# The sample's queries meet their states in eight columns per sequence, its scores in 64 columns

## The chip, the core and the metric

The kernel runs on one core of one Trainium2 chip. The metric is the device time of one execution in microseconds (us); the time of a kernel is the median of several runs. On a core several engines work side by side, each through its own instruction stream in order: TensorE (PE; its weight loads, PEld, are told apart from its matmuls in the profile), VectorE (DVE), ScalarE (ACT), GpSimd (POOL) and SyncE (SP), which here issues the DMA transfers. They wait for each other by semaphores.

## The reference: what is computed

One layer of a decoder, for a prompt of 2048 tokens and for a sample of 8 sequences with 8 new tokens each, with the same weights: a norm, one input projection, two kinds of linear recurrence (four heads of retention, four heads of HGRN2, all 128 x 128), a norm and a gate for each head, an output projection, a squared-ReLU MLP, and a last norm. The recurrences work chunk by chunk:

```python
b = jnp.cumsum(gb, axis=2)
...
A = jnp.einsum('bhtd,bhsd,bhtsd->bhts', qb, kb, decay)
o = jnp.einsum('bhts,bhsv->bhtv', A, vb) + jnp.einsum('bhtd,bhdv->bhtv', qb * jnp.exp(b), S)
...
S_new = S * jnp.exp(b_last[:, :, 0, :])[..., None] + jnp.einsum('bhsd,bhsv->bhdv', k_dec, vb)
```

An output has two terms: the scores of a token against the tokens of its own chunk, times their values, and its query times the state from before the chunk. The prompt starts from a state of zeros and hands it on from chunk to chunk. Each sample sequence starts from a state of its own (`state_ret`, `state_hgrn`: 8 sequences x 4 heads of 128 x 128 for each kind), which its 8 tokens alone meet; its scores are those of its 8 tokens among themselves.

## The kernel before

**Groups.** The tokens go through in three groups, `GROUPS`: 512 of the prompt; the 64 of the sample with 768 of the prompt; 768 of the prompt. Only the second has sample tokens (`g.ns` = 64), in columns 0 to 63 of its 832; features lie on the partitions. For each group come the mixer (`mix`: for each of the four heads p the gates of the head before, then `project`, `mixer`, `values`), the output projection and the MLP.

**Precision.** The large matmuls split each operand in two parts (hi, lo) of a reduced type and take three products; `cut` and `parts` make the parts on ACT (L359, L498) and DVE (L360, L499). The matmuls of the recurrence take 32-bit operands as they are; in the profile each such matmul stands as two weight loads and two matmuls, called passes here.

**Tiles.** `slab` is a pool of 42 buffers of 128 x 832, from which nearly all intermediate results come (`get`); `ld` are six buffers that DMA fills. In PSUM there are two double banks `pj` for projections and four banks `mm` (which also hold `po`, the outputs of the heads). A buffer is given out again when its last reader is done, and its next writer waits for that.

**Order.** `tick()` is called after every few projection matmuls, and runs what is due by then. `mixer` puts the recurrence's steps on that agenda, so that they stand between the projection's matmuls in TensorE's stream. From the order in which the program is written, the framework's scheduler makes the final order of each engine's stream and gives out buffers; so an edit can move instructions that it does not name.

**The sample's part, for each of the four heads of the second group.** Retention's scores: `ret_scores(2)` multiplies all 128 first columns of keys and queries (L962) into a bank and masks them on DVE with a table that is zero outside the sample (L963). HGRN2's: `kept(i, ..., 2)` does the same for the level of 4 tokens (L850, L851); other levels come from shared sums (`own`, `next_to`, `quad`). `turn` transposes keys (L788) and empties the bank on ACT (L790, or with a scale L792). `sample_load` fetches four states in each of two `ld` buffers (L744), and `sample_queries` copies the queries: `g.qm` are two slabs, set to zero once at the start of `mix` (L618); sequence s has 128 columns, of which its 8 queries fill those of its own tokens (columns 8 s to 8 s + 7), and the rest stay zero. `sample_out` adds nine matmuls into the bank `po`: the values times the scores (L756), and for each sequence its state times its 128 columns (L759). As the columns of other sequences are zero, the sum puts each sequence's term in its own place. `sample_update` then makes the new states (L770 on DVE, L773 on PE, L777 or L779 and L780), and they are stored (L781). Other lines named below: `exponents`, `decays` and `decayed` (L832, L833, L837, L843, L844), `corners` (L913, which use a part of the array's columns), `values` (L727), projections (L352), `residual` (L1159).

## Time and profile before

| | us |
|---|---|
| median of 3 runs | 2588.03 |
| lowest and highest run | 2586.77, 2589.51 |
| the profiled execution | 2586.12 |
| its span, first to last instruction | 2584.3 |
| TensorE matmuls busy in the span | 2538.6 |
| VectorE, ScalarE, GpSimd busy | 1688.4, 1166.5, 772.3 |

The profile is of one execution. Matmul rows of the trace name the output and inputs, the part of the array that is used (128*128 is all: rows*columns), and the output's size. Matmuls are pipelined: a row's length is not the time that the matmul takes from the next one. The distance of starts tells that, and a weight load that starts late shows that PE had to wait for something. Where an engine idles, the row in brackets says how long and what ended it.

### The profile page before, as it was taken

What the parts mean: (1) busy time and instruction counts of PE and PEld (TensorE: products, weight loads), DVE (VectorE), ACT (ScalarE), POOL (GpSimd) and SP (SyncE); (2) the same over time, 40 slices, a digit from 0 to 9 for tenths busy, and PEclk for the clock granted to TensorE, in tenths of its full rate; (3) what the DMA queues carried; (4) which work ended last, traced back from release to release, by engine and by line L of the source; (5) the groups of instructions that cost most, each with busy time, mean ns of one, the idle gap of its engine ahead of it and who ended that gap; (6) DMA issues with size and microseconds to landing.
All of it is one profiled execution on the core that took longest, in us unless ns stands there. A gap on an engine that the chain in (4) does not pass through costs nothing. (4 is left out here: it accounts for less than half of the span.)

```text
span 2584.3 us, 37190 instructions
## 1 busy us (share of the span) xinstructions
PE 2538.6 (98%) x14689; PEld 2404.1 (93%) x14689; DVE 1688.4 (65%) x2122; ACT 1166.5 (45%) x1575; POOL 772.3 (30%) x480
## 2 busy tenths in 40 slices
PE   8999999999999999999999999999999999999997
PEld 6888788888999999999999999999999999999997
DVE  6666776556666576646655977875556465559886
ACT  6666533234434343345434444454444354345443
POOL 5655251111234143201222322242244012223222
PEclk9999999999999999999999999999999999999999
DMA  7556755554264655613456555442222325565452
GB/s 256 207 201 210 279 202 195 192 195 161 98 220 158 225 202 170 230 72 136 167 169 228 206 174 177 149 160 82 99 108 100 120 90 179 183 218 194 171 180 82
DMA packets 146237, 442.33 MB, mean 171 GB/s; under 512 B 14736, under 2 KB 36240, under 8 KB 146064
## 3 DMA queue, kind: packets, MB, share of 16 engines
q1 hardware_dynamic: 145920, 439.94, 48.8%
q8 instruction: 116, 1.90, 0.3%
q14 instruction: 57, 0.47, 0.1%
q10 hardware_dynamic: 144, 0.02, 0.0%
HBM read 331.11 MB, written 108.79 MB: 170 GB/s over the span
## 5 line engine op out<-in xcount | busy, mean ns | idle before, releaser
L352 PE MATMUL pj<-slab,hi 128*128 128x416 f32 (+2 forms) x2844 | 742.4, 364 | 6.3 <-ACT hi L277 5.9
L277 ACT CAST hi<-raw 128x1024 fp32r<-128x1024 f32 x330 | 346.7, 1051 | 677.9 <-PE pu L1145 191.6
L292 POOL TENSOR_TENSOR lo<-raw,hi 128x1024 fp32r<-128x1024 f32 x119 | 314.7, 2645 | 933.9 <-ACT hi L277 866.4
L352 PEld LDWEIGHTS pj<-slab,hi 128*128 128x128 f32 x2844 | 514.3, 189 | 39.1 <-ACT hi L277 5.9
L1145 PE MATMUL pd<-slab,hi 128*128 128x416 f32 (+1 forms) x1792 | 469.5, 342 | 5.1 <-DVE slab L1588 3.1
L352 PE MATMUL pj<-slab,lo 128*128 128x416 f32 (+2 forms) x1422 | 435.6, 364 | 0.1
L1145 PE MATMUL pu<-slab,hi 128*128 128x416 f32 (+1 forms) x1600 | 408.1, 342 | 0.0
L292 DVE TENSOR_TENSOR lo<-raw,hi 128x1024 fp32r<-128x1024 f32 x211 | 269.5, 1277 | 188.7 <-ACT hi L277 188.2
L1145 PEld LDWEIGHTS pd<-slab,hi 128*128 128x128 f32 x1792 | 329.4, 188 | 8.7 <-DVE slab L1588 3.7
L1145 PE MATMUL pd<-slab,lo 128*128 128x416 f32 (+1 forms) x896 | 307.9, 344 | 0.0
L1145 PEld LDWEIGHTS pu<-slab,hi 128*128 128x128 f32 x1600 | 294.0, 188 | 1.5
L352 PEld LDWEIGHTS pj<-slab,lo 128*128 128x128 f32 x1422 | 259.9, 189 | 17.2 <-issue 1.9
L1145 PE MATMUL pu<-slab,lo 128*128 128x416 f32 (+1 forms) x800 | 264.2, 343 | 0.0
L352 PE MATMUL mm<-slab,hi 128*128 128x512 f32 x740 | 229.5, 390 | 0.0
L727 PE MATMUL pjv<-hi,slab 128*128 128x256 f32 x1088 | 211.9, 286 | 1.0 <-ACT slab L737 1.0
L1344 DVE TENSOR_TENSOR slab<-slab 128x832 fp32r<-128x832 f32 (+1 forms) x144 | 162.9, 1148 | 37.4 <-ACT slab L1340 18.1
L727 PEld LDWEIGHTS pjv<-hi,slab 128*128 128x128 f32 x1088 | 174.2, 190 | 3.0 <-ACT slab L737 1.4
L1340 ACT CAST slab<-slab 128x832 fp32r<-128x832 f32 (+1 forms) x144 | 122.0, 860 | 116.7 <-DVE slab L1351 83.1
L1145 PEld LDWEIGHTS pd<-slab,lo 128*128 128x128 f32 x896 | 168.1, 188 | 0.5
L352 PEld LDWEIGHTS mm<-slab,hi 128*128 128x128 f32 x740 | 138.5, 188 | 29.2 <-ACT slab L1175 0.4
L727 PE MATMUL pjv<-lo,slab 128*128 128x256 f32 x544 | 153.8, 283 | 0.0
L1145 PEld LDWEIGHTS pu<-slab,lo 128*128 128x128 f32 x800 | 149.7, 188 | 0.5
(205 smaller groups left out, 3708.3 us busy)
## 6 DMA issues: line engine op xcount, KB each, us to landing
raw<-w SPq DMA_DIRECT2D x270, 512.0 KB, 4.1
u<-ld SPq DMA_DIRECT2D x32, 416.0 KB, 4.2
slab<-u SPq DMA_DIRECT2D x32, 416.0 KB, 5.7
u<-ld SPq DMA_DIRECT2D x32, 384.0 KB, 4.6
slab<-u SPq DMA_DIRECT2D x32, 384.0 KB, 4.9
ld<-x SPq DMA_DIRECT2D x16, 416.0 KB, 4.8
ld<-x SPq DMA_DIRECT2D x16, 384.0 KB, 4.0
raw<-su1S SPq DMA_DIRECT2D x8, 512.0 KB, 3.9
```

The source lines that it names most:

```text
L277: self.nc.scalar.copy(hi, raw)
L292: eng.tensor_tensor(out=lo, in0=self.second.pop(j), in1=hi.bitcast(F32), op=ALU.subtract)
L352: self.nc.tensor.matmul(pj[:, i, :T2], w, a[:, c0:c1], start=j == 0 and q == 0, stop=j == n - 1 and q == 2)
L727: nc.tensor.matmul(pj[:, i * 256:(i + 1) * 256], a[:, s:s + C], ww, start=kb == 0 and q == 0, stop=kb == KB - 1 and q == 2)
L1145: self.nc.tensor.matmul(*a, **k)
L1340: self.nc.scalar.copy(hi[:, :g.T], B[name][:, :g.T])
L1344: self.nc.vector.tensor_tensor(out=lo[:, :g.T], in0=B[name][:, :g.T], in1=hi.bitcast(F32)[:, :g.T], op=ALU.subtract)
```

## The change

The mixer's slabs of zeros `g.qm`, their memsets and `sample_queries` are gone. `sample_out` takes the queries where they are: for each sequence one matmul of its state (128 columns of weights, as before) with its 8 query columns, into the 8 columns of `po` that are its own. The first matmul of `sample_out` takes the 64 sample tokens alone: 64 partitions of values and scores, 64 columns. The two kinds of scores, L850 and L962, are made for 64 x 64, and masked on 64 partitions and 64 columns. The number of matmuls stays the same. The line numbers in this document are those of the kernel before, for both kernels, unless it says otherwise.

```diff
@@ mix
-        if g.ns:
-            g.qm = [self.get(), self.get()]
-            for q in g.qm:
-                nc.gpsimd.memset(q, 0.0)
@@ sample_queries, sample_out
-    def sample_queries(self, g, q):
-        for i in range(2):
-            z = g.qm[i][:, 32 * i:32 * i + 4 * 136].rearrange("p (s r) -> p s r", r=136)[:, :, 0:SLEN]
-            self.nc.gpsimd.tensor_copy(z, q[:, 32 * i:32 * i + 32].rearrange("p (s r) -> p s r", r=SLEN))
-
-    def sample_out(self, g, po, v, AT, s0):
+    def sample_out(self, po, v, AT, s0, q):
         nc = self.nc
-        nc.tensor.matmul(po[:, 0:P], v, AT, start=True, stop=False)
-        for i in range(2):
-            for s in range(4):
-                nc.tensor.matmul(po[:, 0:P], s0[i][:, s * P:(s + 1) * P], g.qm[i][:, s * P:(s + 1) * P],
-                                 start=False, stop=i == 1 and s == 3)
+        nc.tensor.matmul(po[:, :NS], v[:NS], AT[:NS, :NS], start=True, stop=False)
+        for s in range(NSEQ):
+            c = slice(s * SLEN, (s + 1) * SLEN)
+            nc.tensor.matmul(po[:, c], s0[s // 4][:, s % 4 * P:(s % 4 + 1) * P], q[:, c], start=False, stop=s == NSEQ - 1)
@@ kept, sg == 2
-                ps = self.mm(P)
-                nc.tensor.matmul(ps, qk[:, :P], qk[:, :P], start=True, stop=True)
-                nc.vector.copy_predicated(self.ATs, msk[:, NLV + i], ps)
+                ps = self.mm(NS)[:NS]
+                nc.tensor.matmul(ps, qk[:, :NS], qk[:, :NS], start=True, stop=True)
+                nc.vector.copy_predicated(self.ATs[:NS, :NS], msk[:NS, NLV + i, :NS], ps)
@@ ret_scores, sg == 2
-                x["ats"] = self.get()[:, :P]
-                ps = self.mm(P)
-                nc.tensor.matmul(ps, rk[:, :P], rq[:, :P], start=True, stop=True)
-                nc.vector.tensor_tensor(out=x["ats"], in0=ps, in1=con[:, C_RS + p * P:C_RS + (p + 1) * P], op=ALU.mult)
+                x["ats"] = self.get()[:, :NS]
+                ps = self.mm(NS)[:NS]
+                nc.tensor.matmul(ps, rk[:, :NS], rq[:, :NS], start=True, stop=True)
+                nc.vector.tensor_tensor(out=x["ats"][:NS], in0=ps, in1=con[:NS, C_RS + p * P:C_RS + p * P + NS], op=ALU.mult)
@@ mixer
         def sample_load(hd):
             x["s0", hd] = self.sample_states(hd, p)
-            self.sample_queries(g, q if hd else rq)
...
-                self.sample_out(g, x["po", 0][0], b["vs"][0], x["ats"], x["s0", 0])
+                self.sample_out(x["po", 0][0], b["vs"][0], x["ats"], x["s0", 0], rq)
...
-                self.sample_out(g, x["po", 0][1], b["vs"][1], self.ATs, x["s0", 1])
+                self.sample_out(x["po", 0][1], b["vs"][1], self.ATs, x["s0", 1], q)
```

## The prediction

> **What bounds the kernel now.** I read the page's head, then the stretch in which the second group is mixed, then TensorE's waits in it. The first fence has the span and busy times of the page and the clock by core; the second the busy time of 640 to 1085 us (columns: length, then busy us and instructions of PE, PEld, DVE, ACT, POOL, clock, DMA share, GB/s); the third what TensorE waited for there (us in all, times, longest).

> ```profile
> span 2584.3 us, 37190 instructions
> PE 2538.6 (98%) x14689; PEld 2404.1 (93%) x14689; DVE 1688.4 (65%) x2122; ACT 1166.5 (45%) x1575; POOL 772.3 (30%) x480
> core 0: 2584.3 us, clock 0.997
> ```
> ```profile
> 640.00:1085.00 445.00, 438.24 (x2849) 419.16 (x2848) 301.44 (x447) 181.63 (x267) 147.20 (x118) 1.00 0.54 185
> ```
> ```profile
> PE mm L505 <- DVE slab L360: 3.3, 2, 1.6
> PE mm L788 <- ACT slab L792: 1.4, 1, 1.4
> PE mm L970 <- DVE AT L877: 1.1, 1, 1.1
> PE pjv L727 <- ACT slab L737: 1.0, 2, 0.6
> ```

> TensorE is the bound: 438.2 of 445.0 us busy at full clock, and the 6.8 us of waits are the four rows. So an edit counts by what it does to the time between matmul starts on PE, and by what it does to those four waits. Work taken from POOL (147 us busy of 445) or DVE (301 of 445) counts only where PE waits for it.

> **What the change touches on POOL, DVE and the queues.** The groups of these lines from 620 to 1090 us (count, then busy us in all, mean ns, idle us before):

> ```profile
> L752 POOL COPY slab<-slab 128x32 f32<-128x32 f32 x16 | 4.8, 315 | 29.7 <-PE po L759 29.1 <-DMA sd11S<-raw 0.3
> L618 POOL MEMSET slab<- 128x832 f32 x2 | 1.5, 791 | 17.6 <-PE mm L352 17.6
> L851 DVE COPY_PREDICATED ATs<-msk,mm 128x128 f32<-128x128 uint8 x4 | 1.2, 295 | 0.0
> L963 DVE TENSOR_TENSOR slab<-mm,con 128x128 f32<-128x128 f32 x4 | 1.2, 292 | 4.8 <-PE mm L962 4.8
> ```

> The 16 copies and two memsets go: 6.3 us of POOL, with 29.7 and 17.6 us idle ahead of them, and no row above has PE waiting for POOL: nothing. The eight DVE instructions on a quarter of the elements save at most their 2.4 us, beside PE: nothing. No DMA is added. In the changed program's order one of the two loads of retention states for each of the second to fourth heads is issued behind the stores of the head before:

> ```profile
> L744 SPq DMA_DIRECT2D ld<-ret_s x8: 378/380/380, 634.2 to 973.2; - x8
> L759 PE MATMUL po<-slab,ld x128: 275/275/275, 752.9 to 1079.3; 128*128 128x128 f32 x128
> ```

> The last of these loads starts at 973 us for a use after 1070: the cover is some 90 us, and a step of a few us is hidden. The two slabs that come free matter for one wait, below.

> **The eight-column matmuls (L759).** Each matmul of this type is two passes, each with its own weight load (128 rows for 64 matmuls). The timeline (start us, length, engine, line, count) of one call in the first head:

> ```profile
> 752.52 0.38 PEld L756 LDWEIGHTS po<-slab 128*128 128x128 f32 x2
> 752.82 1.87 PEld L759 LDWEIGHTS po<-slab,ld 128*128 128x128 f32 x16
> 754.60 0.30 PEld L352 LDWEIGHTS pj<-slab,lo 128*128 128x128 f32 x2
> ```

> From 752.82 to the next line's load at 754.60 are 1.78 us for 16 passes: 0.111 us each. The change cuts the moving columns from 128 to 8, and leaves the weights at 128 columns. Whether a pass can be shorter than 0.111 depends on what a weight load takes when nothing hides it. The corners (L913) show it, the one place where the array works on fewer columns (128*64 and 128*32 against 128*128):

> ```profile
> 714.93 0.28 PE L727 MATMUL pjv<-hi,slab 128*128 128x256 f32 x1
> 715.14 0.42 PEld L913 LDWEIGHTS mm<-slab 128*64 128x64 f32 x6
> 715.63 0.19 PEld L727 LDWEIGHTS pjv<-hi,slab 128*128 128x128 f32 x1
> 715.63 0.39 PE L727 MATMUL pjv<-hi,slab 128*128 128x256 f32 x1
> 715.74 0.19 PEld L727 LDWEIGHTS pjv<-lo,slab 128*128 128x128 f32 x1
> 715.85 0.28 PE L727 MATMUL pjv<-lo,slab 128*128 128x256 f32 x1
> ...
> 721.13 0.45 PEld L913 LDWEIGHTS mm<-slab 128*32 128x32 f32 x12
> ```
> ```profile
> L913 PE MATMUL mm<-slab 128*32 128x32 f32 x256 | 13.3, 204 | 3.0 <-DVE slab L971 3.0
> L913 PEld LDWEIGHTS mm<-slab 128*32 128x32 f32 x256 | 10.6, 117 | 10.2 <-issue 5.2 <-DVE slab L971 3.4 <-ACT slab L837 0.3
> L913 PEld LDWEIGHTS mm<-slab 128*64 128x64 f32 x128 | 9.2, 137 | 5.0 <-issue 1.8 <-DVE slab L844 1.1
> ```

> At 715.63 a load of 128 columns starts with the array empty. Its matmul is recorded 0.39 long instead of 0.28, and the load after it starts at 715.74: 0.11 us of bare load. With one length of a load taken off, the passes of 64 columns are (0.42 - 0.137) / 5 = 0.057 us apart, those of 32 (0.45 - 0.117) / 11 = 0.030. The corners move as many columns as they load, so these two alone don't tell load from stream; the bare load does. Bounds of the new pass: 0.030 (stream alone) to 0.111; I take 0.108, by the bare load of the same 128 columns. 128 x (0.111 - 0.108) = 0.4 us saved, at most 128 x 0.081 = 10.4 us.

> [...]

> **The 64-wide scores (L850, L962).** Their output is now 64 partitions, so the array works as 128*64 for two passes, amid 128*128 work. The fence above shows what such a visit costs: the small load waits until 715.14, 0.21 after the matmul before it started (its recorded 0.28 less 0.07), where a load of the same shape would start at once; and the first full load, at 715.63, comes 0.15 after the last small matmul (715.14 + 6 x 0.057 = 715.48); then 0.11 of bare load. The lines as they are now:

> ```profile
> 722.32 0.28 PE L727 MATMUL pjv<-hi,slab 128*128 128x256 f32 x1
> 722.33 0.31 PEld L962 LDWEIGHTS mm<-slab 128*128 128x128 f32 x2
> 722.67 0.19 PEld L727 LDWEIGHTS pjv<-lo,slab 128*128 128x128 f32 x1
> ```
> ```profile
> 742.04 0.54 PE L352 MATMUL pj<-slab,lo 128*128 128x416 f32 x2
> 742.24 0.37 PEld L850 LDWEIGHTS mm<-slab 128*128 128x128 f32 x2
> 742.53 0.30 PEld L352 LDWEIGHTS pj<-slab,hi 128*128 128x128 f32 x2
> ```
> ```profile
> L352 PE MATMUL pj<-slab,hi 128*128 128x416 f32 x820 | 200.8, 358 | 0.0
> ```

> L962, from the matmul before it to the start of the full matmul behind it: now 722.67 - 722.32 = 0.35 us. Then 0.21 (drain) + 2 x 0.057 (passes) + 0.15 (drain) + 0.11 (bare load) = 0.58: 0.23 more, four times, 0.9 us. L850 stands behind a matmul of 416 columns, recorded 0.36, so its drain is 0.36 - 0.07 = 0.29. These matmuls start 0.18 apart (0.54 - 0.36): now 0.18 + 2 x 0.111 = 0.40, then 0.29 + 2 x 0.057 + 0.15 + 0.11 = 0.66: 0.26 more, four times, 1.0 us. The halved loads alone would save 16 x (0.111 - 0.057) = 0.9 us; that is the other end.

> **The first matmul of each call (L756).** It now contracts over 64 partitions, and the built program sets the array to 64*128 for it. No row has such a shape. Lower bound: no drain, two passes of 0.108, nothing. Upper: drained like the corners, on the way in and out: 0.29 + 0.11 + 0.11 + 0.15 + 0.11 = 0.77 against 0.40, or 0.37 more, eight times, 3.0 us. I take the upper end, since both partial shapes that the trace has (64 and 32 columns) drain both ways.

> [...]

> **One wait.** In the fourth head:

> ```profile
> 1046.66 0.90 ACT L837 ACTIVATE slab<-slab 128x832 f32<-128x832 f32 x1 [2.04 <-POOL slab L833]
> 1047.63 1.01 DVE L360 TENSOR_TENSOR slab<-slab 128x832 fp32r<-128x832 f32 x1
> 1048.67 1.37 ACT L792 ACTIVATE slab<-mm,con 128x384 f32<-128x384 f32 x3 [1.11 <-DVE slab L360]
> 1049.31 0.33 PE L788 MATMUL mm<-con,slab 128*128 128x128 f32 x1 [1.43 <-ACT slab L792]
> ```

> L792 cannot write its slab until L360 has read it, so the bank it empties comes free late, and L788 holds PE for 1.43 us. In the changed program's order the first two L792 stand ahead of L837 and wait for PE alone, no longer for DVE: another slab. L788 also moves seven projection matmuls ahead. I take the whole 1.4 us as gained; the ends are that and a loss (third rival). The other three waits keep their instructions in order, so they stay. Of the other moves, L777 now stands behind L1159 on DVE in the fourth head; the second pair of L773 that needs L777's banks is moved back too, so nothing.

> **Sum.** -0.4 + 0.9 + 1.0 + 3.0 - 1.4 = +3.1 us. On the span 2584.3 that is 2587.4, on the profiled execution's 2586.1 it is 2589.2. The median of the runs, 2588.0, lies 1.9 above that execution, so I predict 2591.1. A measurement tells about 0.2%, 5.2 us, from no change: this is no change, on the slow side.

> **Rivals.**
> Short passes are cheap: if a pass of eight columns went at the corners' 0.030, 10.4 us would go instead of 0.4: 2581.1, faster. For it: the corners. Against it: the bare 0.11 at 715.63. [...] 6%.
> The 64-row shape doesn't drain: 3.0 us less, 2588.1. For it: no row shows rows changing. 18%.
> L792 still waits for L360's slab (slower): then L788, now 7 x 0.18 = 1.3 us earlier, holds PE for 2.7 instead of 1.4 us; the sum is +4.5 + 1.3 = +5.8, 2593.8. It decides from the point where L792 starts no more than 0.6 us (5.8 - 5.2) earlier than now. Against it: the order just told. 14%, and 6% that the wait merely stays: 2592.5.
> Every short pass drains the one before: a pass waits the recorded 0.20 of a short matmul less 0.07, then 0.11 for its load, so 0.24 instead of 0.11: 128 x 0.13 = 17 us, 2608. Against it: 0.030 between the 32-column passes. 4%.
> The forecast has 45%; the last 7% are waits that I don't see, half of them past the bound.

> Faster 6%; slower 14 + 4 + some 4 = 22%; within 0.2% the other 72%. The range runs from 2585.5, below the second rival, to 2594.5, above the third.

> **What would show it.** Right: L759 loads still some 0.11 us apart; gaps of 0.2 to 0.3 us ahead of the loads of L756, L850 and L962, and 0.15 behind them; L788's wait gone. Wrong: L759's 16 passes well under 1.7 us, no gap at L756, or PE waiting for L792, L777 or a state load.

## The result, and the profile after

The changed kernel took 2594.01 us (median of 8 runs, 2592.21 to 2595.97), the kernel before 2587.28 (8 runs, 2586.33 to 2592.84) beside it. The ratio is 1.0023, with a 95% interval of 1.0014 to 1.0033: slower by 0.23%, a little past the 0.2% that I called no change. The forecast was 2591.1; the range to 2594.5 holds the result, with 0.5 us to spare. One of the eleven executions of split_near, further down, ran at a granted clock of 0.751 and took 3131.8 us; it is the profiled one, so the clock of that kernel is read from a second run of it, split_near_look.

The head of the page and the clock of the changed kernel:

```profile
span 2593.4 us, 37153 instructions
PE 2550.3 (98%) x14689; PEld 2409.6 (93%) x14689; DVE 1670.7 (64%) x2122; ACT 1166.6 (45%) x1575; POOL 771.9 (30%) x462
core 0: 2593.4 us, clock 0.994
```

PE has the same 14689 matmuls in 9.1 us more of span, and is still 98% busy; DVE and POOL do less, and it gives nothing. New is the mean granted clock: 0.994, where it was 0.997.

These are TensorE's waits in the second group's mix, 640 to 1085 us (us in all, times, longest). In this kernel's own numbering L723 is L727 of before, L733 is L737, L961 is L970 and L868 is L877; below, L748 and L751 are L756 and L759, L764 is L773, L779 is L788, and L783 would be L792.

```profile
PE pjv L723 <- ACT slab L733: 2.1, 3, 1.1
PE mm L505 <- DVE slab L360: 2.0, 2, 1.6
PE mm L961 <- DVE AT L868: 1.4, 1, 1.4
```

The wait of L788 for L792 is gone, as forecast. The other three have moved a little against each other and come to 5.5 us (5.4 before).

One call of the second head on the weight-load side, in the changed kernel (start us, length, count):

```profile
861.09 0.38 PEld L352 LDWEIGHTS pj<-slab,hi 128*128 128x128 f32 x2
861.47 0.44 PEld L779 LDWEIGHTS mm<-con,slab 128*128 128x128 f32 x3
861.88 0.30 PEld L352 LDWEIGHTS pj<-slab,hi 128*128 128x128 f32 x2
862.45 0.29 PEld L748 LDWEIGHTS po<-slab 64*128 64x128 f32 x2 [0.28 <-PE mm L779]
862.81 1.86 PEld L751 LDWEIGHTS po<-slab,ld 128*128 128x128 f32 x16
864.60 0.44 PEld L352 LDWEIGHTS pj<-slab,lo 128*128 128x128 f32 x2
865.05 0.68 PEld L352 LDWEIGHTS pj<-slab,hi 128*128 128x128 f32 x2
865.75 0.22 PEld L779 LDWEIGHTS mm<-con,slab 128*128 128x128 f32 x1
```

and the same call before the change:

```profile
858.72 0.30 PEld L352 LDWEIGHTS pj<-slab,hi 128*128 128x128 f32 x2
859.02 0.38 PEld L756 LDWEIGHTS po<-slab 128*128 128x128 f32 x2
859.32 1.87 PEld L759 LDWEIGHTS po<-slab,ld 128*128 128x128 f32 x16
861.10 0.30 PEld L352 LDWEIGHTS pj<-slab,lo 128*128 128x128 f32 x2
```

Three things are to be read from these. The load of L756 has an idle time of 0.28 us ahead of it: from the load of L352 in front it starts 862.45 - 861.88 = 0.57 us later, against 859.02 - 858.72 = 0.30 before. The 64-row shape drains in this trace: the load does not overlap the matmuls in front of it as that of the full shape did. The 16 passes of eight columns take 864.60 - 862.81 = 1.79 us, 0.112 each, against 861.10 - 859.32 = 1.78 with 128 columns: nothing is saved. And behind the call two loads of L352 take 0.68 us (at 865.05), where two of the same kind took 0.38 ahead of it (at 861.09). That last is not in my sum at all. This table by stretch (length, busy us and instructions of PE, PEld, DVE, ACT, POOL, then the granted clock) shows what it is:

```profile
640.00:1085.00 445.00, 439.54 (x2808) 415.96 (x2807) 280.53 (x442) 182.91 (x268) 146.12 (x100) 0.99 0.52 180
861.29:864.70 3.41, 3.41 (x27) 3.01 (x25) 3.41 (x11) 1.25 (x3) 0.00 (x0) 1.00 0.76 310
864.70:868.11 3.41, 3.41 (x12) 3.15 (x12) 0.48 (x1) 0.27 (x1) 0.00 (x0) 0.50 0.02 5
871.53:874.94 3.41, 3.41 (x25) 3.28 (x25) 0.83 (x1) 0.00 (x0) 1.85 (x2) 1.00 0.61 186
874.94:878.35 3.41, 3.41 (x7) 1.38 (x5) 0.69 (x1) 0.00 (x0) 0.20 (x1) 0.50 0.42 154
1076.33:1079.74 3.41, 3.41 (x27) 3.01 (x26) 3.04 (x7) 2.42 (x4) 0.00 (x0) 1.00 0.00 0
1079.74:1083.15 3.41, 3.41 (x12) 3.17 (x11) 1.67 (x3) 0.27 (x1) 0.00 (x0) 0.50 0.02 5
```

Three times TensorE ran for one stretch of 3.41 us at a granted clock of 0.50, each time directly behind a stretch that holds a whole call. Before the change this part had none: its 1.00 alone would not tell, as one such stretch in 445 us takes off only 0.004, but the trace's record of the granted clock has no half clock between 249 and 2576 us. At 0.50, a stretch of 3.41 us loses at most 1.7 us; the two traces, laid on each other instruction by instruction, give about 1.6 for each. From the same alignment, the profiled executions differ by: the eight calls +2.8 (0.35 each), L962 +0.22 and L850 +0.24 for each of four visits (+1.8), the wait of L788 -1.6, the three half-clock stretches +4.8, +1.0 ahead of this part, where half-clock stretches fell otherwise on work that the change doesn't touch, and some 0.3 in small shifts: 9.1 us. The medians differ by 6.7.

### The profile page after: what moved, and what is told of

It is laid out like the page before. It is cut to its first block, busy times and chain, and to the rows that moved or that the text cites. A ratio compares the mean times of both kernels' runs of the same rounds, so it can differ in the third digit from the quotient of the medians.

```text
span 2593.4 us, 37153 instructions
## 1 busy us (share of the span) xinstructions
PE 2550.3 (98%) x14689; PEld 2409.6 (93%) x14689; DVE 1670.7 (64%) x2122; ACT 1166.6 (45%) x1575; POOL 771.9 (30%) x462
## 5 line engine op out<-in xcount | busy, mean ns | idle before, releaser
L352 PE MATMUL pj<-slab,hi 128*128 128x416 f32 (+2 forms) x2844 | 745.4, 365 | 6.7 <-ACT hi L277 6.3
L352 PEld LDWEIGHTS pj<-slab,hi 128*128 128x128 f32 x2844 | 516.8, 190 | 40.6 <-ACT hi L277 6.3
L352 PE MATMUL pj<-slab,lo 128*128 128x416 f32 (+2 forms) x1422 | 437.7, 366 | 0.0
L352 PEld LDWEIGHTS pj<-slab,lo 128*128 128x128 f32 x1422 | 260.8, 190 | 17.4 <-issue 2.2
L352 PE MATMUL mm<-slab,hi 128*128 128x512 f32 x740 | 229.6, 390 | 0.0
L723 PE MATMUL pjv<-hi,slab 128*128 128x256 f32 x1088 | 212.3, 287 | 2.1 <-ACT slab L733 2.1
L723 PEld LDWEIGHTS pjv<-hi,slab 128*128 128x128 f32 x1088 | 174.3, 190 | 4.6 <-ACT slab L733 2.7
L352 PEld LDWEIGHTS mm<-slab,hi 128*128 128x128 f32 x740 | 138.5, 188 | 29.2 <-ACT slab L1165 0.5
L723 PE MATMUL pjv<-lo,slab 128*128 128x256 f32 x544 | 153.8, 283 | 0.0
```

Source lines behind the costliest of these rows:

```text
L352: self.nc.tensor.matmul(pj[:, i, :T2], w, a[:, c0:c1], start=j == 0 and q == 0, stop=j == n - 1 and q == 2)
L723: nc.tensor.matmul(pj[:, i * 256:(i + 1) * 256], a[:, s:s + C], ww, start=kb == 0 and q == 0, stop=kb == KB - 1 and q == 2)
```

## The experiments

Theory A: the partial shapes drain as the prediction priced them, the moved order is harmless, and what comes on top is the half clock that follows some calls. Theory B: the partial shapes alone make all of the loss, and the half clock is chance. Theory C: the eight-column passes, or the instructions that changed places, cost time themselves. All comparisons stand beside runs of the kernel before on the same chip: 2588.8 us in the first and third group of runs, 2588.7 in the second. The line numbers are those of before.

### Full shapes, partial shapes alone, eight columns alone, both calls together

*full_shape*: the change, but scores and L756 use the whole array again.

```diff
-        nc.tensor.matmul(po[:, :NS], v[:NS], AT[:NS, :NS], start=True, stop=False)
+        nc.tensor.matmul(po[:, :NS], v, AT[:, :NS], start=True, stop=False)
...
-                ps = self.mm(NS)[:NS]
-                nc.tensor.matmul(ps, rk[:, :NS], rq[:, :NS], start=True, stop=True)
+                ps = self.mm(NS)
+                nc.tensor.matmul(ps, rk[:, :P], rq[:, :NS], start=True, stop=True)
...
```

> The changed kernel, but the two kinds of scores load all 128 columns of weights (L850, L962) and the first matmul of each call (L756) contracts over all 128 partitions: the array stays 128*128 throughout; moving columns stay 64 and 8. Theory A (the loss is drains at the shape changes, about 4.6 us, plus 3.4 us windows of half clock wherever a call of L756 and L759 falls whole into one of the clock's windows, less the L788 wait): no late loads at L756, L850, L962; the calls shorten from 2.14 to about 2.0 us, so at most one or two windows of half clock in the stretch; 2 us below the kernel before, up to 1.5 above it if two windows stay. Theory B (drains are all of it, the windows of half clock are chance): 2 us below before. Theory C (the eight-column passes or the moved instructions cost the time): still 3 us or more above before.

*shapes_alone*: the kernel before, with only the partial shapes of the change; the slabs of zeros and the 128 moving columns stay.

```diff
-        nc.tensor.matmul(po[:, 0:P], v, AT, start=True, stop=False)
+        nc.tensor.matmul(po[:, 0:P], v[:NS], AT[:NS], start=True, stop=False)
...
-                nc.tensor.matmul(ps, qk[:, :P], qk[:, :P], start=True, stop=True)
+                nc.tensor.matmul(ps, qk[:, :NS], qk[:, :P], start=True, stop=True)
...
```

> The kernel before, with its slabs of zeros, its 128 moving columns and its order, and only the partial shapes of the change: L850 and L962 with 64 columns of weights, L756 over 64 partitions. Theory A: drains only, 4 x 0.33 + 4 x 0.36 + 8 x 0.42 = 6.1 us above before (passes of 128 columns take longer to drain than those of 64), no window of half clock between 640 and 1085 us. Theory B: at least 6 us above before as well. Theory C: nothing, within 1 us of before. If row shapes don't drain: 2.8 us above before.

*eight_alone*: the kernel before; L759 takes from the slabs of zeros only the eight columns of its sequence.

```diff
-                nc.tensor.matmul(po[:, 0:P], s0[i][:, s * P:(s + 1) * P], g.qm[i][:, s * P:(s + 1) * P],
-                                 start=False, stop=i == 1 and s == 3)
+                c = 32 * i + 8 * s
+                nc.tensor.matmul(po[:, c:c + SLEN], s0[i][:, s * P:(s + 1) * P], g.qm[i][:, s * P + c:s * P + c + SLEN], start=False, stop=i == 1 and s == 3)
```

> The kernel before, but L759 moves only the 8 columns of each slab of zeros that are the sequence's own, into its 8 columns of the bank; memsets, copies, slabs and shapes as before. Theory A: passes stay 0.111 us apart, so no gain; call low for 1.8 us, which is less than the 2.1 us that brought a window of half clock and less than the 1.9 that did not: 0 to 1 window; within 2 us of before. Theory B: within 0.5 us of before. Theory C: 3 us or more above before. If short passes were cheap: 8 to 10 us below before.

*calls_together*: full_shape, with the two calls of a head back to back.

```diff
-            at(t + 6, sample_load, 1)
-            at(t + 10, sample, 1)
+            at(t - 12, sample_load, 1)
+            at(t + 1, sample, 1)
```

> full_shape with the two calls of each head back to back (the second one's states loaded earlier): 32 short passes and two first matmuls in a row, about 4 us, with the same work and no partial shape. Theory A: in each of the four heads the 4 us cover at least 2 us of some window of 3.41 us, so four windows of half clock, 1.6 us each: 6 to 7 us above full_shape. Theories B and C: within 1 us of full_shape.

| | us | ratio to before, 95% interval | half-clock stretches, 640 to 1085 us |
|---|---|---|---|
| full_shape | 2585.77 | 0.9991 (0.9982 to 1.0000) | 0 |
| shapes_alone | 2595.07 | 1.0026 (1.0016 to 1.0037) | 0 |
| eight_alone | 2588.59 | 1.0001 (0.9992 to 1.0010) | 1 |
| calls_together | 2593.22 | 1.0022 (1.0014 to 1.0031) | 4 |

Theory C falls with eight_alone and full_shape: neither eight moving columns nor the new order costs the 3 us or more that it asked for. One call of eight_alone (its L760 is L759):

```profile
859.60 0.37 PEld L756 LDWEIGHTS po<-slab 128*128 128x128 f32 x2
859.89 1.87 PEld L760 LDWEIGHTS po<-slab,ld 128*128 128x128 f32 x16
861.68 0.30 PEld L352 LDWEIGHTS pj<-slab,lo 128*128 128x128 f32 x2
```

The 16 passes take 861.68 - 859.89 = 1.79 us, with 128 moving columns 1.78: the number of moving columns changes nothing. A pass then takes 0.112 us, against 0.11 for the bare load of 128 columns of weights (715.63 to 715.74 in the corners' rows). That run had one stretch at half clock, not behind a call but behind the wait of L788, 1.9 us here:

```profile
1048.38:1051.79 3.41, 1.52 (x12) 1.36 (x11) 3.41 (x4) 2.15 (x4) 0.60 (x1) 1.00 0.84 339
1051.79:1055.20 3.41, 3.41 (x15) 3.32 (x14) 0.91 (x2) 0.00 (x0) 0.00 (x0) 0.50 0.68 205
```

The drains are confirmed by shapes_alone: +6.3 us with no half clock in this part of its profile (mean granted clock 0.997 over that execution), and an interval (4.1 to 9.6) that holds its expected 6.1 and the 4.6 of the change's drains, and not the 2.8 that was expected if rows don't drain. Its L756 shows the same late load, with 128 columns moving:

```profile
861.98 0.29 PEld L756 LDWEIGHTS po<-slab 64*128 64x128 f32 x2 [0.28 <-PE mm L788]
862.39 1.86 PEld L759 LDWEIGHTS po<-slab,ld 128*128 128x128 f32 x16
```

The half clock without any drain is confirmed by calls_together: 7.4 us more than full_shape, which has the same matmuls in other places; four stretches at 1.6 us come to 6.4. So Theory B falls too: half clock isn't chance here, and drains are not all. In calls_together the double calls are 4.1 us of short passes, and stretches behind them run at half clock:

```profile
754.39:757.80 3.41, 3.41 (x29) 3.40 (x30) 1.03 (x2) 0.00 (x0) 1.43 (x2) 1.00 0.01 2
757.80:761.22 3.42, 3.42 (x10) 2.56 (x9) 0.00 (x0) 0.27 (x1) 0.63 (x1) 0.50 0.00 0
```

The four are not one for each head, as was expected: the third head has two, one right behind the other, and the second head none, although 2.21 us of its double call lie in one stretch. So the 2 us that the expectation took as enough were not enough here without drains.

### The changed kernel again, its calls cut in two, and longer calls without drains

*change_again* is the changed kernel, *split_near* and *split_far* cut each call: in two halves with two projection matmuls between them (split_near), or with ten or eleven passes of full matmuls (split_far).

```diff
-        nc.tensor.matmul(po[:, :NS], v[:NS], AT[:NS, :NS], start=True, stop=False)
-        for s in range(NSEQ):
+        half or nc.tensor.matmul(po[:, :NS], v[:NS], AT[:NS, :NS], start=True, stop=False)
+        for s in range(4 * half, 4 * half + 4):
...
-            at(t + 1, sample, 0)
+            at(t + 1, sample, 0, 0); at(t + 2, sample, 0, 1)
...
-            at(t + 10, sample, 1)
+            at(t + 10, sample, 1, 0); at(t + 11, sample, 1, 1)
```

In split_far the second halves stand at t + 6 and t + 15, and the updates of the states behind them. *longer_full* is full_shape with L756 made twice, the second time added on.

> The changed kernel once more, for another position of its calls (L756 and L759, 2.14 us each) against the windows of 3.41 us in which the clock is granted. Theory A (a call that lies in one window with 2.1 us or more is followed by a window at half clock): such windows stand only behind such calls, each costs about 1.6 us; some 2 or 3 of the 8 calls, and about 2594 us, with 2592 to 2596. Theory B (the extra windows of the first profile were chance): none or as many at other places, and about 2591 by the drains alone.

> The changed kernel with each call cut in two halves of some 1.0 us, two matmuls of 416 columns (0.36 us) between them; drains and all else stay. Theory A, if the sum of the short passes in a window counts: a window that holds all of a call (2.5 us long now) is still followed by one at half clock, about 2 of 8, and about 2593 us. Theory A, if it is one unbroken stretch that counts: no half clock in the mix of the second group, and 2589 to 2590. Theory B: the same as the changed kernel, about 2594.

> As the one before, but the halves are some 2 us or more apart, so that no window of 3.41 us holds much more than half a call of short passes; the states are updated somewhat later. Theory A either way: no window at half clock in the mix of the second group, and the drains alone are left, 2589 to 2591 us. Theory B: about 2594.

> The version without partial shapes (full_shape, 2585.8), with the first matmul of each call (L756) made twice, so that a call lasts about 2.30 instead of 2.08 us without any drain. It adds the values times the scores twice, so the sample's output differs from the reference. By its passes alone: 8 x 0.22 = +1.8 us, 2587.6. Theory A, if the length of the call is the cause whatever its shape: some 3 of the 8 calls lie in one window with 2.1 us or more, each followed by half clock at 1.6 us: about +6 to +7, 2592 to 2593. If the drains are needed for it: 2587.6 and no half clock in the mix of the second group.

| | us | ratio to before, 95% interval | half-clock stretches, 640 to 1085 us |
|---|---|---|---|
| change_again | 2594.89 | 1.0024 (1.0015 to 1.0033) | 3 |
| split_near | 2593.15 | 1.0016 (1.0007 to 1.0025) | see split_near_look |
| split_far | 2590.18 | 1.0005 (0.9996 to 1.0014) | 0 |
| longer_full | 2587.46 | 1.0001 (0.9992 to 1.0010) | 0 |

In change_again the calls lay otherwise against the stretches of 3.41 us, and again exactly the calls that fell whole into one were followed by half clock: those at 861.49, 976.95 and 1076.37 us. The other five had at most 1.93 us in one stretch.

```profile
860.58:863.99 3.41, 3.41 (x27) 3.01 (x26) 3.41 (x10) 0.99 (x3) 0.00 (x0) 1.00 0.79 323
863.99:867.40 3.41, 3.41 (x12) 3.17 (x11) 0.23 (x1) 0.27 (x1) 0.00 (x0) 0.50 0.02 5
976.64:980.05 3.41, 3.41 (x26) 3.06 (x25) 0.00 (x0) 0.00 (x0) 1.60 (x2) 1.00 0.65 192
980.05:983.46 3.41, 3.41 (x8) 1.82 (x6) 0.69 (x1) 0.00 (x0) 0.46 (x1) 0.50 0.47 153
```

In split_far the same matmuls, with the same partial shapes, had the full clock throughout this part, and the trace's record has no half clock between 250 and 2581 us (mean granted clock 0.997 over the execution, 0.994 in change_again):

```profile
640.00:1085.00 445.00, 440.10 (x2837) 416.80 (x2835) 286.13 (x446) 183.03 (x268) 147.36 (x101) 1.00 0.53 182
```

It took 2594.89 - 2590.18 = 4.7 us less, which is what three stretches of 1.6 us come to. So the half clock is worth about 4.7 of the changed kernel's 6.2 us on this chip, though each of the two medians is known to some 2.3 us only. What is left, 1.5 us with an interval of -1.0 to 3.6, has room for the 3.0 that the drains less the wait of L788 leave by the rows.

longer_full missed. A call of 2.30 us is longer than the changed kernel's 2.14, three lay whole in one stretch, and none was followed by half clock (the stretch behind the one from 859.71 us has 1.00); the time is that of its passes alone, 2587.5 against 2587.6. The length of a call alone, with which I had begun, does not sort these runs.

### split_near again, still longer calls, the scores alone, the slabs held

*split_near_look* is split_near again, for its profile. *longest_full* is full_shape with L756 made three times.

```diff
-        nc.tensor.matmul(po[:, :NS], v, AT[:, :NS], start=True, stop=False)
+        nc.tensor.matmul(po[:, :NS], v, AT[:, :NS], start=True, stop=False); nc.tensor.matmul(po[:, :NS], v, AT[:, :NS], start=False, stop=False); nc.tensor.matmul(po[:, :NS], v, AT[:, :NS], start=False, stop=False)
```

*scores_alone* is the change with L756 over 128 rows, and zeros in the rows that it adds; only the scores stay partial.

```diff
-        nc.tensor.matmul(po[:, :NS], v[:NS], AT[:NS, :NS], start=True, stop=False)
+        nc.tensor.matmul(po[:, :NS], v, AT[:, :NS], start=True, stop=False)
...
+                nc.gpsimd.memset(x["ats"][NS:], 0.0)
```

*slabs_held* is full_shape with the two slabs taken as before.

```diff
+        if g.ns:
+            g.qm = [self.get(), self.get()]
+            for q in g.qm:
+                nc.gpsimd.memset(q, 0.0)
...
         def sample_state(hd):
+            for z in g.qm:
+                nc.gpsimd.memset(z[:, :SLEN], 0.0)
```

> The kernel of split_near again (2593.2 us), for a profile of its clock: its time is that of the changed kernel less 1 to 2 us. If the sum of short passes and drains in a window counts, a window at half clock stands behind each window of 3.41 us that has about 2.2 us or more without full matmuls, and behind no other: 0 to 3 of them; if only an unbroken stretch counts, none, and something else makes up the 3 us above split_far.

> As longer_full, with L756 made three times: a call of 2.52 us, again without any drain (and a sample's output that differs from the reference, as the scores' term is added three times). In longer_full whole calls of 2.30 us, 2.16 of them without full matmuls, were not followed by half clock; in the changed kernel 2.22 and 2.27 with the drains were. If the time without full matmuls counts, however it comes about, calls that lie whole in a window have 2.4 here and are followed by half clock: some 3 of 8, and 8 x 0.44 + 3 x 1.6 = +8 on full_shape, about 2594 us, with 2591 to 2596. If it takes the drains, none is, and 2585.8 + 3.5 = 2589.3.

> The changed kernel with the first matmul of each call (L756) on all 128 rows of the array (the rows of the scores past the 64th are set to zero on POOL); only the scores L850 and L962 keep their partial shape. On full_shape (2585.8): 4 x 0.22 + 4 x 0.24 = +1.8 us by the drains, 2587.6; calls of 2.08 us as in full_shape, so no half clock in the mix of the second group. If the windows at half clock came with the scores' drains: 2592 or more.

> The version without partial shapes (full_shape, 2585.8), but the two slabs stay taken through the mix (set to zero as before, and written once for each call on POOL, beside other work), so 40 slabs go round as before the change, not 42. If the freed slabs took away the wait of L788 for L792 in the fourth head: it comes back with 1.4 to 1.9 us, and 2587.5. If it was the order that the instructions got without the copies: no such wait, and 2585.8.

| | us | ratio to before, 95% interval | half-clock stretches, 640 to 1085 us |
|---|---|---|---|
| split_near_look | 2593.03 | 1.0017 (1.0007 to 1.0027) | 2 |
| longest_full | 2590.53 | 1.0008 (1.0000 to 1.0017) | 0 |
| scores_alone | 2589.34 | 1.0001 (0.9993 to 1.0010) | 0 |
| slabs_held | 2585.61 | 0.9988 (0.9979 to 0.9996) | 0 |

split_near_look: two calls lay whole in one stretch, their halves 0.3 us apart, and both were followed by half clock. So it need not be one unbroken run of short passes: two halves in one stretch were enough.

```profile
761.11 0.29 PEld L756 LDWEIGHTS po<-ATs,slab 64*128 64x128 f32 x2 [0.28 <-issue]
761.48 0.97 PEld L759 LDWEIGHTS po<-slab,ld 128*128 128x128 f32 x8
762.36 0.30 PEld L352 LDWEIGHTS pj<-slab,lo 128*128 128x128 f32 x2
762.67 1.05 PEld L759 LDWEIGHTS po<-slab,ld 128*128 128x128 f32 x8
```
```profile
760.77:764.18 3.41, 3.41 (x26) 3.06 (x25) 0.00 (x0) 0.00 (x0) 1.34 (x2) 1.00 0.65 196
764.18:767.59 3.41, 3.41 (x8) 1.83 (x6) 0.69 (x1) 0.00 (x0) 0.76 (x1) 0.50 0.45 150
```

longest_full came out at 2590.5, near the 2589.3 of its passes, and without half clock:

```profile
968.53:971.94 3.41, 3.41 (x29) 3.40 (x28) 3.05 (x10) 0.85 (x2) 0.00 (x0) 1.00 1.01 354
971.94:975.35 3.41, 3.41 (x16) 2.39 (x14) 1.06 (x2) 0.27 (x1) 0.00 (x0) 1.00 0.50 202
```

Here 2.53 us of a call lie in the first stretch, as in three others of this kernel (2.47 to 2.53), and the clock stays. So the time without full matmuls, as I had put it after longer_full, does not sort them either: with drains 2.14 us of call were enough, without them 2.53 us were not, but in calls_together 2.62, 2.73 and 2.78 us were. With the 0.28 us of idle time ahead of L756's load added, the changed kernel's calls come to 2.42 us, which is still less than 2.53. The matmuls that longer_full and longest_full add move 64 columns, not eight, but the sum of the columns moved in each stretch doesn't sort all of them: the stretch of longest_full from 1081.17 us, which kept the clock, has matmuls of 2592 columns in all, and that of the changed kernel from 871.53, which lost it, has 2752. No run isolates the condition, and it stays open.

scores_alone had no half clock, so the scores' drains alone don't bring it. It came 1.7 us above its expectation, within what these medians can tell; its own trace shows one wait that full_shape's hasn't, L913 for DVE, 1.1 us. slabs_held has no wait of L788:

```profile
PE pjv L727 <- ACT slab L737: 2.3, 3, 1.1
PE mm L505 <- DVE slab L360: 2.0, 2, 1.6
PE mm L970 <- DVE AT L877: 1.4, 1, 1.4
```

With 40 slabs to go round, as before, the wait is gone all the same: the freed slabs did not take it away. In shapes_alone and eight_alone, which keep the copies and the old order, it is there with 1.9 us. slabs_held and full_shape are level; they are the best versions found, some 3 us or 0.1% better than before, though the interval of full_shape reaches 1.0000. The wait of L788, 1.4 to 1.9 us, is a part of that gain; where the rest comes from is not shown.

## Why the prediction was right, and what it lacked

By the steps of the sum:

- *The eight-column passes*, -0.4 us: right that the fewer moving columns bring nearly nothing. The passes stayed at 0.112 us instead of 0.108, so nothing was saved; the 0.108 was my estimate off the bare load, whose rows show 0.11. The first rival (0.030) and the fourth (0.24) fall by the same row.
- *The scores*, +0.9 and +1.0: 0.22 and 0.24 measured for a visit, 0.23 and 0.26 forecast. This is L962 in change_again:

```profile
722.86 0.28 PE L727 MATMUL pjv<-hi,slab 128*128 128x256 f32 x1
723.07 0.19 PEld L962 LDWEIGHTS mm<-slab 128*64 128x64 f32 x2
723.33 0.19 PEld L727 LDWEIGHTS pjv<-hi,slab 128*128 128x128 f32 x1
723.33 0.39 PE L727 MATMUL pjv<-hi,slab 128*128 128x256 f32 x1
723.43 0.19 PEld L727 LDWEIGHTS pjv<-lo,slab 128*128 128x128 f32 x1
```

  The small load starts 723.07 - 722.86 = 0.21 us after the matmul in front, and behind it stands 0.10 us of bare load (723.33 to 723.43): the gaps that the corners had shown, at the sizes that they had shown. L850, behind a matmul of 416 columns, starts 0.28 us late:

```profile
742.62 0.38 PEld L352 LDWEIGHTS pj<-slab,lo 128*128 128x128 f32 x2
743.27 0.19 PEld L850 LDWEIGHTS mm<-slab 128*64 128x64 f32 x2 [0.28 <-DVE slab L924]
```
- *L756's shape*, +3.0: it drains. From load to load around the call are 864.60 - 861.88 = 2.72 us against 861.10 - 858.72 = 2.38, so 0.34 more where 0.37 were forecast (0.35 each over the eight calls, +2.8). The second rival (no drain for rows) falls. The trace has 0.28 us of idle ahead of the load.
- *The wait of L788*, -1.4: gone, -1.6. The cause that I gave was half wrong: the two slabs that came free did not take it away, since it is gone with the slabs held. The order that the prediction told of (the first two L792 ahead of L837, in the fourth head) stands in all eleven profiles without the wait, and in the three with it, those of the kernel before, shapes_alone and eight_alone, L837 comes first; that the order alone does it was not isolated. The third rival (L792 still late) falls.
- *Missing: the half clock.* The terms above add up to +3.0 us measured, against +3.1 forecast. On top come about 4.7 us from three stretches at half clock. I had read the granted clock, 1.00 in this part, as a fact about the chip rather than as something that this change could move: I priced each pass by its distance from the next, and what a call of short passes, 2.14 of the 3.41 us of a stretch, does to the clock of the next stretch was not considered. Together the five terms are +7.7 us; the medians differ by 6.7, with an interval of 3.6 to 8.5, so they fit, and the last 1 us is not accounted for. The third rival's 2593.8 lies close to the result by accident; its mechanism did not occur.

So the forecast was right that the change gains nothing and costs a little, and near in the size of its four steps; it was 2.9 us low because a fifth was missing, worth more than the four together. The miss would have been larger but for the kernel before, which came out 0.75 us faster beside the change (2587.28) than the 2588.03 that the forecast was added to. That the range held is luck: its upper end was put up for the third rival. And by its own line of 0.2% the result, 0.23%, lies on the slower side, to which it had given 22%. Idle time of TensorE did not announce the three half-clock stretches of the changed kernel: in the stretches ahead of them the matmul rows have no idle time (3.41 of 3.41 us busy) and the weight-load rows at most 0.28 us at a time, and the clock was halved all the same.

## What to carry to other kernels

Cutting the moving columns of these matmuls gained nothing: with 128 columns of weights a pass took 0.111 to 0.112 us, for 128 moving columns and for eight. Cutting the weights or the rows to a part of the array cost a drain on each side, 0.22 to 0.35 us in all for a visit amid full matmuls. The cheap half of such an edit can be kept alone: with full shapes the change was some 3 us better than before instead of 6 us worse. And a long run of short passes had a second price here that no row of it shows, some 1.6 us for each stretch at half clock; what exactly brings it is open. So look at the granted clock of the stretches behind such a run, and if it falls, try the passes spread out among full matmuls, as in split_far, which took 4.7 us less.

## What the runs showed of the hardware that I had not expected

| kernel | us of calls in one stretch | followed by half clock |
|---|---|---|
| the change, two profiles | 2.14, six times, with a drain | 6 of 6 |
| the same | 1.93 and less | none |
| split_near_look | 2.52, with two full matmuls and a drain in it | 2 of 2 |
| the same | 2.27 and less | none |
| full_shape | 2.08 and 2.09, no drain | none |
| eight_alone, scores_alone, slabs_held | 2.05 to 2.09, nine times, no drain in the call | none |
| longer_full | 2.30, 2.31, 2.30, 2.16, no drain | none |
| longest_full | 2.47 to 2.53, four times, no drain | none |
| calls_together | 2.62, 2.73, 2.78, no drain | 3 of 3 |
| the same | 2.21 and less | none |
| shapes_alone | 2.19, twice, 128 columns, with drains | none |

The last row tells most: with the same drains and nearly the same length, but 128 columns moving, the clock stayed full, twice in one profile. In the changed kernel the eight columns saved no time in their own rows (1.79 us for 16 passes, 1.78 before), and together with the drains they were followed by half clock in the rows behind them.
